# Attention scores in three fp32r products, and GLA's state-times-query product likewise in two of three token blocks

## The chip, the core and the metric

The kernel runs on one core of one Trainium2 chip. TensorE (PE) multiplies 128-row tiles into PSUM, VectorE (DVE) and ScalarE (ACT) do elementwise work and empty PSUM, GpSimd (POOL) does a little elementwise work, and SyncE (SP) issues most transfers. The metric is the device time of one execution in microseconds; lower is better.

## The reference

One layer of a decoder for 2048 new prompt tokens and 8 sequences of 8 sample tokens, width 1024, in fp32. One projection gives the inputs of two branches: grouped attention in a window of 128 with a learned sink, and gated linear attention (GLA) with a recurrent state. The branches are gated, merged, projected and normalised. The two places that matter here:

```python
# attention: 8 heads of 64 in 2 kv groups; a block of 128 queries sees 256 keys
s = jnp.einsum('bnqhgd,bnkhd->bnhgqk', qb, kband).astype(jnp.float32) * (HEAD_DIM ** -0.5)
s = s + rel_bias(rel_table, dist)
...
p = sink_softmax(s, mask, sink...)
o = jnp.einsum('bnhgqk,bnkhd->bnqhgd', p.astype(v.dtype), vband)

# GLA: 4 heads, keys of 128, values of 256, chunk by chunk
o_inter = jnp.einsum('bthk,bhkv->bthv', qt, S)
A = jnp.where(causal, jnp.einsum('bthk,bshk->bhts', qt, kt), 0.0)
o_intra = jnp.einsum('bhts,bshv->bthv', A, vc)
S = jnp.exp(b_last)[..., None] * S + jnp.einsum('bshk,bshv->bhkv', kend, vc)
```

## The kernel before

**Passes.** The big projections run as passes of products 128 by 128 by 352, several with Strassen's seven products in place of eight. Their operands are split into a high part, rounded to fp32r, and a low part, the fp32r rest (`split`: a copy on ACT, L142, and a subtraction on DVE, L143). Three fp32r products then stand for one fp32 product: high by high (L1326), high weight by low input (L1327), low weight by high input (L1328). The tokens go in three stages of 704. In stage 0 the weight operands are made and partly stored; later stages load many of them ready-made.

**Order.** PE's order is written out by hand: the groups of the passes follow each other, four steps of three products make a "tick", and other work is put between the groups by the tick in which it is due (`at`, `tick`). DVE, ACT, POOL and SP get their order from a scheduler that takes work as it falls due and hands out buffers from pools.

**Attention** runs per stage over blocks of 128 queries, seven ticks apart. For a block due at tick o: at o-7 its keys and values (`att_load`, L740, tile `kk`) and queries (`att_q`, L748, tile `zq` of tag `zs`) are loaded by SP; at o-3 `att_prep` transposes the values on PE (L763) and copies them out on DVE (L765); at o `att_scores` runs twice, for two of four query groups each. Its products are plain fp32 with 64 rows: kv group 0 on rows 0 to 63 of the array, kv group 1 on rows 64 to 127 (L777). The results are scaled and biased on DVE (L780). At o+5 `att_sil` loads the output gate (L756, tag `zs`), at o+6 `att_trans` transposes the probabilities (L809; copied out at L811 and L813), and at o+9 `att_out` multiplies by the values (L823), gates the result and stores it (L826). Block 0 sees 128 keys, the other fifteen 256. After the last block the sample tokens follow: `samp_load` takes two tiles of tag `zs`, and `samp_q` (L853) one more for the scaled query that L897 and L898 read.

**GLA** runs per stage over heads and chunks of 256 or 128 tokens, in tiles of 128. For a chunk whose first tile is due at b: `gla_load` at b-13, decays at b-8 (`gla_z`), operands at b-3 (`gla_kq`; the query times the decay is `gb`, L1060), and for each tile `gla_v` and `gla_a` when it is due, `gla_b` 5/3 of a tile's spacing later, `gla_c` 10/3 later. In `gla_b` the tile's output starts as state times query, one fp32 product of 128 rows by 256 columns (L1110, for the 60 of 64 tiles that have a state already), then six fp32r products follow (L1104): the state's increment and the part inside the chunk. DVE then makes the new state (L1118).

**Shared buffers.** Every sink of a pass takes its results from tag `fin`, ten buffers of 352 columns; so do the gates' input and the four `zg` tiles of a gate, which live for nine ticks (products at L711). PSUM has four banks for the passes (`pd`) and four for the rest (`pa`).

Of the kernel before, what the change touches and what calls it, by code (L numbers as in the profile page):

```python
# [12 lines left out]
F32 = mybir.dt.float32  # L13
# [8 lines left out]
P = 128  # L22
# [3 lines left out]
TS = 8  # L26
# [3 lines left out]
G = 4  # L30
# [27 lines left out]
def kernel(ctx, tc, io):  # L58
# [37 lines left out]
    def mt(tag, n, bufs, dt=F32, name=None):  # L96
        return M["p"].tile([P, n], dt, tag=tag, name=name or tag, bufs=bufs)
# [26 lines left out]
    def at(t, fn):  # L124
        side.setdefault(max(int(t), now[0]), []).append(fn)
# [15 lines left out]
    def split(dst_h, dst_l, src, eng=nc.vector):  # L141
        pin["a"] = nc.scalar.copy(dst_h, src)  # L142
        i = eng.tensor_tensor(dst_l, src, dst_h.bitcast(F32), ALU.subtract)  # L143
        if eng is nc.vector:
            pin["d"] = i
# [588 lines left out]
    def att_load(b):  # L734
        t0 = b * W
        k0 = 0 if b else W
        A = AS[b] = {"k0": k0}
        need(z_kv, range(2), max(t0 - W, 0), t0 + W)
        kk = A["kk"] = mt("kk", 4 * W, 2).rearrange("p (a t) -> p a t", a=2)
        nc.sync.dma_start(kk[:, :, k0:], z_kv[:, :, t0 - W + k0:t0 + W])  # L740

    def att_q(b):
        t0 = b * W
        for z in z_q:
            need(z, range(2), t0, t0 + W)
        q = AS[b]["zq"] = mt("zs", G * W, 4, name="zq").rearrange("p (g t) -> p g t", g=G)
        for j in range(2):
            nc.sync.dma_start(q[:, 2 * j:2 * j + 2], z_q[j][:, :, t0:t0 + W])  # L748

    def att_sil(b):  # L750
        t0 = b * W
        for z in z_ga:
            need(z, range(2), t0, t0 + W)
        q = AS[b]["sil"] = mt("zs", G * W, 4, name="sil").rearrange("p (g t) -> p g t", g=G)
        for j in range(2):
            nc.sync.dma_start(q[:, 2 * j:2 * j + 2], z_ga[j][:, :, t0:t0 + W])  # L756

    def att_prep(b):
        A = AS[b]
        k0 = A["k0"]  # L760
        tp = pa()
        for i in range(k0 // W, 2):
            nc.tensor.transpose(tp[:, i * P:(i + 1) * P], A["kk"][:, 1, i * P:(i + 1) * P], ident)  # L763
        vt = A["vt"] = mt("vt", 2 * P, 2).rearrange("p (b c) -> p b c", c=P)
        nc.vector.tensor_copy(vt[:, k0 // W:].rearrange("p b c -> p (b c)"), tp[:, k0:2 * P])  # L765

    def att_scores(b, g0):
        A = AS[b]
        k0 = A["k0"]
        if g0 == 0:  # L770
            for kv in range(2):
                A["s", kv] = w4(name="s").rearrange("p (g k) -> p g k", g=G)
        ps = [pa().rearrange("p (a k) -> p a k", a=2) for _ in range(2)]
        for j in range(2):
            for kv in range(2):
                r = slice(kv * HD, (kv + 1) * HD)
                mm(ps[kv][:, j, k0:], A["zq"][r, g0 + j, :], A["kk"][r, 0, k0:], start=True, stop=True,  # L777
                   tile_position=(kv * HD, 0))
        for kv in range(2):
            nc.vector.scalar_tensor_tensor(A["s", kv][:, g0:g0 + 2, k0:], ps[kv][:, :, k0:], HD ** -0.5,  # L780
                                           st1["bias", kv][:, g0:g0 + 2, k0:], ALU.mult, ALU.add)
        if g0 == 0:
            return
        nm, sm, es, rd = (small([P, NH], n) for n in ("nm", "sm", "es", "rd"))
        for kv in range(2):
            nc.vector.tensor_reduce(nm[:, kv * G:(kv + 1) * G], A["s", kv][:, :, k0:], AX.X, ALU.max, negate=True)
        nc.vector.tensor_tensor(nm, nm, nsink, ALU.min)
        for h in range(NH):
            sl = A["s", h // G][:, h % G, k0:]
            nc.scalar.activation(sl, sl, AF.Exp, bias=nm[:, h:h + 1], accum_out=sm[:, h:h + 1])  # L790
# [40 lines left out]
    def samp_load():  # L831
        for z in [z_kv] + z_q + z_ga:
            need(z, range(2), NP, NT)
        SA["kv"] = mtile("fin", name="skv")[:, :2 * NS].rearrange("p (a t) -> p a t", a=2)
        SA["kw"] = mtile("fin", name="kw")[:, :W]
        nc.sync.dma_start(SA["kv"], z_kv[:, :, NP:])
        nc.sync.dma_start(SA["kw"], z_kv[:, 0, NP - W:NP])
        SA["zq"], SA["sil"] = (mt("zs", G * W, 4, name=n)[:, :G * NS].rearrange("p (g t) -> p g t", g=G) for n in ("szq", "ssl"))
        for j in range(2):
            nc.sync.dma_start(SA["zq"][:, 2 * j:2 * j + 2], z_q[j][:, :, NP:])  # L840
            nc.sync.dma_start(SA["sil"][:, 2 * j:2 * j + 2], z_ga[j][:, :, NP:])
        kc = w4(name="kc").rearrange("p (b c) -> p b c", b=NB)
        vc = w4(name="vc").rearrange("p (b c) -> p b c", b=NB)
        nc.sync.dma_start(kc, io["ck"].rearrange("b w c -> w b c"))
        nc.sync.dma_start(vc, io["cv"].rearrange("b w c -> w b c"))
        SA["kc"], SA["vc"] = kc, vc
        nc.sync.dma_start(io["o_ks"][:, 0:W - TS, :], io["ck"][:, TS:W, :])
        nc.sync.dma_start(io["o_vs"][:, 0:W - TS, :], io["cv"][:, TS:W, :])

    def samp_q():  # L850
        qs = SA["qs"] = mt("zs", G * W, 4, name="qs")[:, :G * NS].rearrange("p (b g t) -> p b g t", g=G, t=TS)
        for g in range(G):
            nc.scalar.mul(qs[:, :, g, :], SA["zq"][:, g].rearrange("p (b t) -> p b t", t=TS), HD ** -0.5)  # L853

# [223 lines left out]
    def gla_a(B, i):  # L1078
        ts = slice(i * P, (i + 1) * P)
        ap = pa()  # L1080
        mm(ap[:, :P], B["k"][:, ts], B["q"][:, ts], start=True, stop=True)  # L1081
        A_ = rot("a")
        nc.vector.copy_predicated(A_, cmask.bitcast(U32), ap[:, :P])
        x = rot("ah")
        split(x[:, :P], x[:, P:], A_, nc.gpsimd)
        B["a", i] = x[:, :P], x[:, P:]

    def gla_norm(B, key, o, n):
# [6 lines left out]
        nc.scalar.mul(on[:n], o, sq[:n])  # L1095
        B["on", key] = on

    def gla_b(B, i):
        ts = slice(i * P, (i + 1) * P)
        gh, gl = B["gv", i]  # L1100

        def three(ps, w, x, start):
            for j, (a, c) in enumerate(((w[0], x[0]), (w[1], x[0]), (w[0], x[1]))):
                mm(ps, a, c, start=start and j == 0, stop=(j == 2))  # L1104

        gv, kT2 = (gh[:, :HV], gl[:, :HV]), (gh[:, HV:], gl[:, HV:])
        S = sstate.get(B["h"])
        op = pa()
        if S is not None:
            mm(op[:, :HV], B["qb"][:, ts], S_t[S], start=True, stop=False)  # L1110
        sp = pa()
        three(sp[:, :HV], kT2, gv, True)
        three(op[:, :HV], B["a", i], gv, S is None)
        Sn = S_free.popleft()
        if S is None:
            nc.vector.tensor_copy(S_t[Sn], sp[:, :HV])
        else:
            nc.vector.scalar_tensor_tensor(S_t[Sn], S_t[S], B["e1"][:, i:i + 1], sp[:, :HV], ALU.mult, ALU.add)  # L1118
            S_free.append(S)
        sstate[B["h"]] = Sn  # L1120
        gla_norm(B, i, op[:, :HV], P)
# [59 lines left out]
    def gla_phase(s, t0, st):  # L1181
# [5 lines left out]
        for h, (c0, T_) in ([(h, c) for c in GCH[s] for h in range(GH)] if s == 1 else  # L1187
                            [(h, c) for h in range(GH) for c in GCH[s]]):
            if True:
                last = c0 + T_ == NT  # L1190
                Tp = T_ - (NS if last else 0)
                nt = Tp // P
                B = dict(h=h, t0=c0, T=T_, Tp=Tp, nt=nt, last=last)
                tt = lambda v: b0 + st * v + 0.01
                b = tt(u)
                at(b - 13, lambda B=B: gla_load(B))
# [388 lines left out]
```

## Time and profile before

| | us |
|---|---|
| median of three runs | 1791.93 |
| lowest, highest run | 1784.84, 1792.70 |
| the profiled execution, its own time | 1783.34 |
| span of its records | 1781.6 |
| idle time of PE by the busy sum | 29.6 |

The profiled execution is one run; its span begins with the first record and ends with the last. Its TensorE clock was granted at 0.997 of full speed on the mean. A group of instructions is named by its line, engine, output and inputs; an fp32 product on PE leaves two records, an fp32r product one, and a transpose one. Matmul records overlap, so a product's cost is read from the spacing of starts or from the chain, not from a record's own length.

### The profile page before, as it was taken

To read this page: it belongs to the slowest core of one execution; us is meant where nothing else is said; L and a number is where in the kernel's file an instruction comes from. 1 tells how busy PE (TensorE), PEld (TensorE's weight loads), DVE (VectorE), ACT (ScalarE), POOL (GpSimd) and SP (SyncE) were. 2 spreads that over 40 slices of the span, in tenths; PEclk is the share of its full clock that TensorE was granted. 3 is DMA by queue.
4 is the path that set the end of the run, shared out by engine and by line. 5 is a ranking of instruction groups with operands and counts; after the bars stand their busy time and mean duration, and the time that the engine had idled before them with its cause. 6 is when DMAs were issued, how large, how long until landed. Compare 5 with 4: busy or idle time off the path is not lost.

```text
span 1781.6 us, 31643 instructions
## 1 busy us (share of the span) xinstructions
PE 1752.0 (98%) x11026; PEld 1644.8 (92%) x11026; DVE 1085.9 (61%) x2146; ACT 851.7 (48%) x2052; POOL 374.5 (21%) x522
## 2 busy tenths in 40 slices
PE   8999999998999999999999999999999999999998
PEld 8999988997999988999999998899999999998887
DVE  6656678778555466547655336635766755536666
ACT  4575656556574365446567334645533432311100
POOL 5345533454111000004211100000123132111111
PEclk9999999999999999999999999999999999999999
DMA  6789966976978987887789798779989978965531
GB/s 216 272 317 332 330 232 224 319 279 207 311 261 279 304 258 231 269 286 228 255 266 319 239 294 279 237 244 318 298 267 244 301 212 223 332 148 194 171 104 54
DMA packets 290911, 452.33 MB, mean 254 GB/s; under 512 B 29213, under 2 KB 210133, under 8 KB 290736
## 3 DMA queue, kind: packets, MB, share of 16 engines
q1 hardware_dynamic: 262896, 415.04, 70.7%
q10 hardware_dynamic: 20464, 26.24, 4.2%
q0 software_dynamic: 7392, 9.04, 3.6%
q8 instruction: 87, 1.43, 0.3%
q14 instruction: 72, 0.59, 0.1%
HBM read 297.52 MB, written 153.57 MB: 253 GB/s over the span
## 4 chain that ended last, share of the span: by engine, by line
PE 74%; DMA 2%; DVE 1%; POOL 1%; ACT 1%; issue 1%; SPq 0%; DVEq 0%; ACTq 0%; POOLq 0%
PE pd L1326 17%; PE pd L1328 17%; PE pd L1327 16%; PE pd L1389 3%; PE pd L1390 3%; PE pd L1391 3%; PE pa L1104 2%; PE pa L1110 1%; PE pa L777 1%; PE pa L823 1%; PE pa L809 1%; PE pa L1127 1%; DMA r<-ug_d 1%; PE pa L1067 1%; PE pa L1081 1%; PE pa L1326 1%
## 5 line engine op out<-in xcount | busy, mean ns | idle before, releaser
L143 DVE TENSOR_TENSOR wp<-ws,wp 128x512 fp32r<-128x512 f32 (+1 forms) x396 | 274.4, 696 | 203.9 <-ACT wp L142 192.9
L142 ACT CAST wp<-ws 128x512 fp32r<-128x512 f32 (+1 forms) x396 | 234.2, 595 | 191.8 <-PE pd L1328 127.7
L348 POOL TENSOR_TENSOR ws<-ws 128x256 f32<-128x256 f32 x162 | 144.1, 918 | 156.5 <-DVE wp L143 103.9
L143 POOL TENSOR_TENSOR ah<-aper,ah 128x128 fp32r<-128x128 f32 x64 | 37.3, 583 | 397.6 <-ACT ah L142 394.4
L384 ACT COPY m<-pd 128x352 f32<-128x352 f32 x146 | 66.1, 454 | 87.2 <-PE pd L1328 80.0
L1390 PE MATMUL pd<-woh,x 128*128 128x512 f32 (+1 forms) x272 | 102.4, 377 | 0.0
L1391 PE MATMUL pd<-wol,x 128*128 128x512 f32 (+1 forms) x272 | 102.4, 377 | 0.0
L1389 PE MATMUL pd<-woh,x 128*128 128x512 f32 (+1 forms) x272 | 102.4, 377 | 0.0
L1326 PE MATMUL pd<-x1h,wp 128*128 128x352 f32 x292 | 96.7, 331 | 2.3 <-DVE fin L405 2.2
L1326 PE MATMUL pd<-x7h,wp 128*128 128x352 f32 x292 | 97.1, 333 | 1.1 <-DVE fin L201 0.9
L1326 PE MATMUL pd<-x3h,wp 128*128 128x352 f32 x292 | 96.8, 331 | 0.3 <-DVE fin L399 0.3
L1326 PE MATMUL pd<-x5h,wp 128*128 128x352 f32 x292 | 96.6, 331 | 0.0
L1326 PE MATMUL pd<-x6h,wp 128*128 128x352 f32 x292 | 96.3, 330 | 0.0
L1326 PE MATMUL pd<-x2h,wp 128*128 128x352 f32 x292 | 96.3, 330 | 0.0
L1326 PE MATMUL pd<-x4h,wp 128*128 128x352 f32 x292 | 96.2, 330 | 0.0
L1328 PE MATMUL pd<-x1h,wp 128*128 128x352 f32 x292 | 94.0, 322 | 0.1
L1328 PE MATMUL pd<-x7h,wp 128*128 128x352 f32 x292 | 94.0, 322 | 0.0
L1328 PE MATMUL pd<-x4h,wp 128*128 128x352 f32 x292 | 93.8, 321 | 0.0
L1328 PE MATMUL pd<-x3h,wp 128*128 128x352 f32 x292 | 93.8, 321 | 0.0
L1327 PE MATMUL pd<-x7l,wp 128*128 128x352 f32 x292 | 93.8, 321 | 0.0
L1328 PE MATMUL pd<-x6h,wp 128*128 128x352 f32 x292 | 93.8, 321 | 0.0
L1328 PE MATMUL pd<-x5h,wp 128*128 128x352 f32 x292 | 93.8, 321 | 0.0
(454 smaller groups left out, 5387.9 us busy)
## 6 DMA issues: line engine op xcount, KB each, us to landing
wp<-wk_w_g SPq DMA_DIRECT2D x96, 512.0 KB
ws<-w_g SPq DMA_DIRECT2D x120, 256.0 KB
wk_w_g<-wp SPq DMA_DIRECT2D x48, 512.0 KB
wp<-wk_w_ra SPq DMA_DIRECT2D x32, 512.0 KB
wp<-wk_w_rg SPq DMA_DIRECT2D x32, 512.0 KB
ws<-w_at SPq DMA_DIRECT2D x53, 256.0 KB
wp<-wk_w_at SPq DMA_DIRECT2D x24, 512.0 KB
ws<-w_pg SPq DMA_DIRECT2D x48, 256.0 KB
```

The costliest lines, as they stand in the source:

```text
L142: pin["a"] = nc.scalar.copy(dst_h, src)
L143: i = eng.tensor_tensor(dst_l, src, dst_h.bitcast(F32), ALU.subtract)
L348: nc.gpsimd.tensor_tensor(o[:, c], x[:, c], y[:, c], op)
L384: nc.scalar.copy(A[i], ps)
L777: mm(ps[kv][:, j, k0:], A["zq"][r, g0 + j, :], A["kk"][r, 0, k0:], start=True, stop=True, tile_position=(kv * HD, 0))
L1104: mm(ps, a, c, start=start and j == 0, stop=(j == 2))
L1326: mm(ps, wh, xh[:, ts], start=first, stop=False, skip_group_check=ch)
L1327: mm(ps, wh, xl[:, ts], start=False, stop=False, skip_group_check=ch)
L1328: mm(ps, wl, xh[:, ts], start=False, stop=(k == q.kh - 1 and not (type(i) is tuple and i[1] == 0)), skip_group_check=ch)
L1389: mm(ps, xh[:, xs], hi, start=(k == 0), stop=False)
L1390: mm(ps, xl[:, xs], hi, start=False, stop=False)
L1391: mm(ps, xh[:, xs], lo, start=False, stop=(k == KT - 1))
```

## The change

Three things change.

1. `att_prep` now splits the block's queries (128 by 512) into `qh` and the rest, which overwrites `zq`, and its keys (128 by 256; 128 by 128 in block 0) into `kh` and the rest, in `kk`. `att_scores` makes three fp32r products in place of one fp32 product, in the order high-high, low query, low key, and in each of the three first kv group 0, then 1. The product of the two low parts is left out.
2. For GLA's stages 0 and 1 (`B["s"] < MS - 1`), `gla_kq` splits the decayed query into two `fin` tiles, `qbh` and `qbl`, which live until the chunk's last `gla_b`. The new `gla_s`, due a third of a tile's spacing after the preceding tile's `gla_b`, splits the head's state into `Sh` and `Sl`. In `gla_b` three fp32r products take the place of L1110. Stage 2 stays as it was.
3. Tag `zs` has three buffers instead of four.

The profile's line numbers move by up to 21 in the changed file.

```diff
     def att_q(b):
-        q = AS[b]["zq"] = mt("zs", G * W, 4, name="zq").rearrange("p (g t) -> p g t", g=G)
+        q = AS[b]["zq"] = mt("zs", G * W, 3, F32R, "zq")
+        v = q.bitcast(F32).rearrange("p (g t) -> p g t", g=G)
...
     def att_prep(b):
+        q = A["zq"]
+        x = mt("qh", G * W, 1, F32R)
+        split(x, q, q.bitcast(F32))
+        A["q"] = [t.rearrange("p (g t) -> p g t", g=G) for t in (x, q)]
+        x, y = mt("kh", 2 * W, 1, F32R), A["kk"][:, 0]
+        split(x[:, k0:], y[:, k0:], y.bitcast(F32)[:, k0:])
+        A["k"] = x, y
         vt = A["vt"] = mt("vt", 2 * P, 2).rearrange("p (b c) -> p b c", c=P)
...
     def att_scores(b, g0):
         for j in range(2):
-            for kv in range(2):
-                r = slice(kv * HD, (kv + 1) * HD)
-                mm(ps[kv][:, j, k0:], A["zq"][r, g0 + j, :], A["kk"][r, 0, k0:], start=True, stop=True,
-                   tile_position=(kv * HD, 0))
+            for n, (x, y) in enumerate(((0, 0), (1, 0), (0, 1))):
+                for kv in range(2):
+                    r = slice(kv * HD, (kv + 1) * HD)
+                    mm(ps[kv][:, j, k0:], A["q"][x][r, g0 + j, :], A["k"][y][r, k0:], start=(n == 0), stop=(n == 2),
+                       tile_position=(kv * HD, 0))
...
     def samp_q():
-        qs = SA["qs"] = mt("zs", G * W, 4, name="qs")[:, :G * NS]...
+        qs = SA["qs"] = mt("zs", G * W, 3, name="qs")[:, :G * NS]...
...
     def gla_kq(B):
+        if B["s"] < MS - 1:
+            B["qs"] = [mtile("fin", F32R, n) for n in ("qbh", "qbl")]
+            split(B["qs"][0][:, :T], B["qs"][1][:, :T], B["qb"][:, :T])
...
+    def gla_s(B):
+        S = sstate.get(B["h"])
+        if S is not None and "qs" in B:
+            B["Ss"] = [mt(n, HV, 1, F32R) for n in ("Sh", "Sl")]
+            split(*B["Ss"], S_t[S])
...
     def gla_b(B, i):
-        if S is not None:
+        if S is not None and "qs" in B:
+            three(op[:, :HV], [q[:, ts] for q in B["qs"]], B["Ss"], True, False)
+        elif S is not None:
             mm(op[:, :HV], B["qb"][:, ts], S_t[S], start=True, stop=False)
...
+                    at(tt(u + i + 1), lambda B=B: gla_s(B))
                     at(tt(u + i + 5 / 3), lambda B=B, i=i: gla_b(B, i))
```

How the instructions stand is shown at three places, before and after; a row has the line, the operation, output and inputs, and the size of the output.

PE at the scores of a block in stage 1, before (its `pa` is a PSUM tile):

```order
L1327 MATMUL pd_75<-x5l,wp 128x352
L1328 MATMUL pd_75<-x5h,wp 128x352
L777 MATMUL pa<-kk,zq 128x256 x8
L1326 MATMUL pd_76<-x5h,wp 128x352
L1327 MATMUL pd_76<-x5l,wp 128x352
```

The scores of a block with 256 keys now:

```order
L786 MATMUL pa<-kh,qh 128x256 x2
L786 MATMUL pa<-kh,zq 128x256 x2
L786 MATMUL pa<-kk,qh 128x256 x2
L786 MATMUL pa<-kh,qh 128x256 x2
L786 MATMUL pa<-kh,zq 128x256 x2
L786 MATMUL pa<-kk,qh 128x256 x2
L1347 MATMUL pd_76<-x3h,wp 128x352
```

Each row x2 is the two kv groups; here `zq` and `kk` are the low parts. Eight fp32 products have become twenty-four fp32r products, of which the last twelve are shown. They stay in one piece between the groups of the passes.

DVE in stage 0 around the copies `pT` that free PSUM ahead of the fourth block's scores, before, with the semaphores each waits for:

```order
L393 TENSOR_TENSOR fin<-m_3121,pd_77 128x352 [waits PE_49]
L395 TENSOR_TENSOR fin<-fin,u_3140 128x352 [waits DVE_49]
L401 TENSOR_TENSOR u_3140<-u_3140,pd_74 128x352 [waits DVE_49,PE_49]
L201 SCALAR_TENSOR_TENSOR fin<-th,fin 128x352 [waits Activation_49]
L402 TENSOR_TENSOR fin<-u_3140,m_3121 128x352 [waits DVE_49]
L143 TENSOR_TENSOR wp<-w_3176,wp 128x512 [waits Activation_49]
L811 COPY pT<-pa 128x512 [waits PE_49] x2
```

And now:

```order
L393 TENSOR_TENSOR fin<-m_3187,pd_77 128x352 [waits PE_49,Activation_49]
L143 TENSOR_TENSOR wp<-ws,wp 128x512 [waits DMAHW7_49,DMAHW6_49,Activation_49]
L143 TENSOR_TENSOR zq<-zq,qh 128x512 [waits DMAHW2_49,DMAHW1_49,Activation_49]
L143 TENSOR_TENSOR kk<-kk,kh 128x256 [waits DMAHW0_49,Activation_49]
L143 TENSOR_TENSOR wp<-ws,wp 128x512 [waits DMAHW3_49,Activation_49]
L395 TENSOR_TENSOR fin<-fin,u_3206 128x352 [waits DVE_49]
L820 COPY pT<-pa 128x512 [waits PE_49]
L401 TENSOR_TENSOR u_3206<-u_3206,pd_74 128x352 [waits DVE_49]
L820 COPY pT<-pa 128x512 [waits PE_49]
```

The two subtractions of the split, which wait for the loads, stand ahead of the copies; L401 has come between them, and L201, L402 and a weight split have moved behind them.

ACT at the sample tokens, where `kcT` and `vn` are copies of transposed cache keys and new values, before:

```order
L813 COPY pT<-pa 128x512 [waits PE_49] x2
L142 CAST wp<-ws 128x512
L853 ACTIVATE qs<-szq 128x8x8 x2
L853 ACTIVATE qs<-szq 128x8x8 [waits DMAHW1_49]
L853 ACTIVATE qs<-szq 128x8x8
L384 COPY m_13779<-pd_74 128x352 [waits PE_49]
```

And now:

```order
L870 COPY kcT<-pa 128x512 [waits DVE_49,PE_49]
L870 COPY kcT<-pa 128x512 [waits PE_49]
L388 COPY u_14546<-pd_77 128x352 [waits PE_49]
L142 CAST wp<-ws 128x512
L862 ACTIVATE qs<-szq 128x8x8 [waits DMAHW5_49,DMAHW4_49,DMAHW6_49,DMAHW3_49,DVE_49]
L862 ACTIVATE qs<-szq 128x8x8 x3
L891 COPY vn<-pa 8x512 [waits PE_49] x2
L388 COPY u_14600<-pd_74 128x352 [waits PE_49]
```

The scaled query has moved from ahead of the cache keys' copies to behind them, and waits for transfers, the last block's store among them.

More of the change, by code (lines that the diff above doesn't have):

```diff
@@ L738, in att_load @@
         need(z_kv, range(2), max(t0 - W, 0), t0 + W)
-        kk = A["kk"] = mt("kk", 4 * W, 2).rearrange("p (a t) -> p a t", a=2)
-        nc.sync.dma_start(kk[:, :, k0:], z_kv[:, :, t0 - W + k0:t0 + W])
+        kk = A["kk"] = mt("kk", 4 * W, 2, F32R).rearrange("p (a t) -> p a t", a=2)
+        nc.sync.dma_start(kk.bitcast(F32)[:, :, k0:], z_kv[:, :, t0 - W + k0:t0 + W])
     def att_q(b):
@@ L745, in att_q @@
             need(z, range(2), t0, t0 + W)
-        q = AS[b]["zq"] = mt("zs", G * W, 4, name="zq").rearrange("p (g t) -> p g t", g=G)
+        q = AS[b]["zq"] = mt("zs", G * W, 3, F32R, "zq")
+        v = q.bitcast(F32).rearrange("p (g t) -> p g t", g=G)
         for j in range(2):
-            nc.sync.dma_start(q[:, 2 * j:2 * j + 2], z_q[j][:, :, t0:t0 + W])
+            nc.sync.dma_start(v[:, 2 * j:2 * j + 2], z_q[j][:, :, t0:t0 + W])
     def att_sil(b):
@@ L753, in att_sil @@
             need(z, range(2), t0, t0 + W)
-        q = AS[b]["sil"] = mt("zs", G * W, 4, name="sil").rearrange("p (g t) -> p g t", g=G)
+        q = AS[b]["sil"] = mt("zs", G * W, 3, name="sil").rearrange("p (g t) -> p g t", g=G)
         for j in range(2):
@@ L762, in att_prep @@
         for i in range(k0 // W, 2):
-            nc.tensor.transpose(tp[:, i * P:(i + 1) * P], A["kk"][:, 1, i * P:(i + 1) * P], ident)
+            nc.tensor.transpose(tp[:, i * P:(i + 1) * P], A["kk"].bitcast(F32)[:, 1, i * P:(i + 1) * P], ident)
+        q = A["zq"]
[5 more added lines that the diff above has]
+        A["k"] = x, y
         vt = A["vt"] = mt("vt", 2 * P, 2).rearrange("p (b c) -> p b c", c=P)
@@ L837, in samp_load @@
         nc.sync.dma_start(SA["kw"], z_kv[:, 0, NP - W:NP])
-        SA["zq"], SA["sil"] = (mt("zs", G * W, 4, name=n)[:, :G * NS].rearrange("p (g t) -> p g t", g=G) for n in ("szq", "ssl"))
+        SA["zq"], SA["sil"] = (mt("zs", G * W, 3, name=n)[:, :G * NS].rearrange("p (g t) -> p g t", g=G) for n in ("szq", "ssl"))
         for j in range(2):
@@ L850, in samp_q @@
     def samp_q():
-        qs = SA["qs"] = mt("zs", G * W, 4, name="qs")[:, :G * NS].rearrange("p (b g t) -> p b g t", g=G, t=TS)
+        qs = SA["qs"] = mt("zs", G * W, 3, name="qs")[:, :G * NS].rearrange("p (b g t) -> p b g t", g=G, t=TS)
         for g in range(G):
@@ L1100, in gla_b, with three @@
         gh, gl = B["gv", i]
-        def three(ps, w, x, start):
+        def three(ps, w, x, start, last=True):
             for j, (a, c) in enumerate(((w[0], x[0]), (w[1], x[0]), (w[0], x[1]))):
-                mm(ps, a, c, start=start and j == 0, stop=(j == 2))
+                mm(ps, a, c, start=start and j == 0, stop=(last and j == 2))
         gv, kT2 = (gh[:, :HV], gl[:, :HV]), (gh[:, HV:], gl[:, HV:])
@@ L1192, in gla_phase @@
                 nt = Tp // P
-                B = dict(h=h, t0=c0, T=T_, Tp=Tp, nt=nt, last=last)
+                B = dict(s=s, h=h, t0=c0, T=T_, Tp=Tp, nt=nt, last=last)
                 tt = lambda v: b0 + st * v + 0.01
```

## The prediction

> **What bounds the kernel now.** I read the page's busy shares first, then the shares of the chain that ended last, then busy time by stretches, and last the chain in order of time.
>
> ```profile
> span 1781.6 us, 31643 instructions
> ...
> PE 1752.0 (98%) x11026; PEld 1644.8 (92%) x11026; DVE 1085.9 (61%) x2146; ACT 851.7 (48%) x2052; POOL 374.5 (21%) x522
> ...
> PE 74%; DMA 2%; DVE 1%; POOL 1%; ACT 1%; issue 1%; SPq 0%; DVEq 0%; ACTq 0%; POOLq 0%
> ```
>
> TensorE is busy for 98% of the span and carries 74% of the chain, so a shorter stream of products should show in the time, and work on DVE and ACT should not. By stretches that is true of most of the program only:
>
> ```profile
> 245.00:277.00 32.00, 27.98 (x164) 23.27 (x163) 24.33 (x43) 17.80 (x45) 14.51 (x16) 0.95 0.57 194
> ...
> 395.00:430.00 35.00, 28.62 (x186) 24.36 (x185) 31.43 (x57) 21.80 (x52) 19.55 (x22) 0.95 0.59 186
> 430.00:600.00 170.00, 170.00 (x1102) 165.98 (x1101) 88.16 (x197) 95.84 (x229) 25.98 (x47) 1.00 0.85 278
> 600.00:1240.00 640.00, 640.00 (x4242) 606.48 (x4241) 366.64 (x762) 347.41 (x888) 53.44 (x91) 1.00 0.83 267
> ```
>
> The columns are the length, then busy time of PE, PEld, DVE, ACT and POOL, the granted clock and DMA. From 430 to 1240 PE has no gap, with DVE and ACT a little over half busy. In two stretches of stage 0 PE goes idle for 4.0 and 6.4 us, the clock falls to 0.95, and DVE is 76% and 90% busy. There the elementwise engines set the pace.
>
> **The change, part by part.** *The scores.* In the chain's pieces, each with its length:
>
> ```profile
> 548.04 0.43 PE pa L1110 x2
> 548.47 0.72 PE pa L1104 x6
> ...
> 653.34 0.16 PE pd L1328
> 653.50 1.93 PE pa L777 x16
> 655.42 0.36 PE pd L1326
> 655.78 0.16 PE pd L1327
> ```
>
> One fp32 product with 256 moving columns (L1110, two records) takes 0.43 us, 0.215 a record. One fp32r product of the same shape (L1104) takes 0.72/6 = 0.12, so three cost 0.36, less than one fp32 product.
>
> ```profile
> L777 PEld LDWEIGHTS pa<-kk,zq x16: 182/187/187, 653.4 to 654.8; 64*128 64x128 f32 x16
> L777 PE MATMUL pa<-kk,zq x16: 376/376/480, 653.4 to 655.0; 64*128 64x256 f32 x16
> ```
>
> A block has eight score products, sixteen records. At 0.215 each they would need 3.4 us one after another; they start within 1.6. So the two kv halves, on rows 0 to 63 and 64 to 127 of the array, run side by side: 8 pairs x 0.216 = 1.73. The remaining 0.20 of the 1.93 is the entry into half-height tiles, and the 0.36 of the next L1326 against 0.16 is the exit. Both stay.
>
> After the change a block has 24 fp32r products, 12 pairs. The trace has no fp32r pair on half-height tiles. If pairs run side by side as here, a block takes 12 x 0.12 + 0.20 = 1.64, 0.29 less; if nothing does, 24 x 0.12 + 0.20 = 3.08, 1.15 more. A pair also needs two weight loads of 128 columns in 0.12 us. The fastest loads in the trace are these:
>
> ```profile
> 649.83 1.75 PE pa L809 x16
> ...
> L937 PEld LDWEIGHTS pa<-p,vn x32: 128/133/133, 1194.4 to 1195.3; 8*64 8x64 f32 x32
> L937 PE MATMUL pa<-p,vn x32: 217/218/238, 1194.4 to 1195.3; 8*64 8x32 f32 x32
> ```
>
> L937 starts 32 loads of 64 columns in 0.9 us, two at a time, so a pair each 0.058; twice the columns would be an estimated 0.116, just inside 0.12. I take the near end, since the rows show pairs side by side in this very place: 15 blocks x 0.29 = **-4.4 us**. Block 0 has 128 moving columns. Before, its 8 pairs cost 0.109 each (L809's 1.75/16, the same 128 columns), 0.87 us. No fp32r row has so few columns: 12 pairs cost from 0.9 (half of 0.12, plus a little) to 2.6 (as an fp32 product, 0.218). I take the load pace, 12 x 0.116 = 1.4: **+0.5**.
>
> *GLA's state product*, 40 tiles of 60: 0.43 becomes 0.36, **-2.9 us**, the rest of the group being fp32r already. So PE's stream is shorter by 6.8 us.
>
> *The splits.* Each is a copy on ACT and a subtraction on DVE, priced by the weight splits:
>
> ```profile
> L142 ACT CAST wp<-ws 128x512 fp32r<-128x512 f32 x348 | 215.2, 622 | 154.0 <-PE pd L1328 90.0 <-POOL ws L348 39.3 <-DMA ws<-w_pg 7.9
> L142 ACT CAST wp<-ws 128x256 fp32r<-128x256 f32 x48 | 19.1, 404 | 37.8 <-PE pd L1328 37.7
> L143 DVE TENSOR_TENSOR wp<-ws,wp 128x512 fp32r<-128x512 f32 x348 | 254.6, 734 | 189.0 <-ACT wp L142 178.0 <-DMA wp<-wk_w_g 2.4 <-DMA wk_w_at<-wp 1.9
> L143 DVE TENSOR_TENSOR wp<-ws,wp 128x256 fp32r<-128x256 f32 x48 | 19.8, 418 | 14.9 <-ACT wp L142 14.9
> ```
>
> A block adds 0.62 + 0.40 = 1.03 us on ACT and 0.73 + 0.42 = 1.15 on DVE; a state split 0.40 and 0.42, and so does a chunk's query. Over 16 blocks, 40 tiles and 24 chunks that is some 42 us on ACT and 45 on DVE. In stages 1 and 2 PE's full row covers them. The state's split is on a chain:
>
> ```profile
> 538.90 0.71 PE pa L1104 x6
> ...
> L1118 DVE SCALAR_TENSOR_TENSOR S<-S,e,pa 128x256 f32<-128x256 f32 x60 | 28.2, 470 | 23.1 <-PE pa L1104 23.0
> ```
>
> The state is ready 0.47 us after 539.6, and its next reader starts at 548.04: 8 us for 0.8 us of work. Nothing, as long as ACT's queue is not 7 us late. The query's split now makes ACT wait for its load, three ticks ahead of the scores:
>
> ```profile
> 257.17 1.42 SPq L748 DMA_DIRECT2D zq<-z_q  x2
> ...
> mg_d<-fin POOLq DMA_DIRECT2D x48, 176.0 KB, 4.8
> ```
>
> This is the latest of these loads. By the page's only row with a landing, 4.8 us, it lands by 263.4, and its scores start at 270.35. Behind ACT's wait stand the copies that free PSUM banks, so I keep it with the next term.
>
> *Stage 0.* Here the cover is missing:
>
> ```profile
> 270.35 0.70 PE L777 MATMUL pa<-kk,zq 64*128 64x256 f32 x2 [1.36 <-ACT pT L813]
> 272.61 3.44 PE L777 MATMUL pa<-kk,zq 64*128 64x256 f32 x14 [1.57 <-DVE pT L811]
> ...
> PE pa L544 <- DVE S L1118: 2.2, 1, 2.2
> ...
> PE pa L1104 <- DVE aper L1083: 2.0, 1, 2.0
> ```
>
> PE waited for the copies that free PSUM ahead of the scores; the 3.44 us for 14 records (1.7 elsewhere) are the lowered clock that followed. The first stretch gets two blocks' splits (2.3 us of DVE), the second three states and two queries (2.1). If all of it falls on the path and trips the clock twice more, at 1.7 us each, it costs 4.4 + 3.4 = 8. But the order of DVE and ACT is dealt anew, and the idle time (4.0 there) with its slow clock (1.7) may go: -6. I take **+2**.
>
> *The small buffers.* The query's halves come from "fin", ten buffers that all sinks share.
>
> ```profile
> 486.28 0.79 PE pa L711 x4
> ...
> 519.88 0.79 PE pa L711 x4
> ```
>
> At L711 the gates of the next stage are made, two per stage, inside GLA's phase. A gate holds five "fin" buffers for nine ticks (a tick is twelve products, 1.92 us). A chunk's halves are held from three ticks ahead of its first tile to 8/3 tiles later; at 9.6 us a tile (538.90 to 548.47) that is some 16 ticks, and a chunk begins every 10: two to four more. One to three are left where two sinks give eight results and four helpers in 14 ticks, each until its store has landed (4.8 us by the row above). DVE or ACT then waits for a landing with PSUM evictions behind it. Before, five were free and PE lost nothing there. A wait of 0 to 3 us at each of four gates: 0 to 12; PE's four banks absorb most, so I take **+2**.
>
> *The samples.* "zs" has three buffers instead of four, so the scaled query (L853) waits for the last block's store.
>
> ```profile
> 1162.45 0.70 ACT L853 ACTIVATE qs<-szq 128x64 f32<-128x64 f32 x4
> ...
> 1170.14 0.56 SPq L826 DMA_DIRECT2D ua_d<-sil  x1
> ...
> 1175.32 0.44 PE L897 MATMUL pa<-kcT,qs 64*32 64x128 f32 x8
> ```
>
> The store issued at 1170.14 lands at 1174.9 by 4.8 us; with 0.70 of scaling the query is ready at 1175.6, against 1175.32: **+0.3** (0 to 2).
>
> Sum: -4.4 + 0.5 - 2.9 + 2 + 2 + 0.3 = **-2.5 us**.
>
> **The rivals.** *(a) The whole gain arrives*: stage 0 and the gates cost nothing. -6.5, and with stage 0's own idle time gone -12. For it: 810 us without a gap on PE. Against: the two stretches above. *(b) Nothing lies side by side in the scores*: a load must wait until the product on its own rows is done, and the other half of the array can't hide it as it is in the same state. A pair then costs 0.116 + 0.12 = 0.236, a block 2.83 + 0.20, 1.1 more, times 15 = +16.5; with the other terms (0.5 - 2.9 + 4.3) the kernel is **18 us slower**. It decides from 1.73/12 = 0.144 us a pair on. Against it: L777's pairs follow at 0.216 with streaming alone at 0.215, so their loads were hidden; for it, only that an fp32r pair leaves half the time. The Trainium skill's page "TensorE: Matmul & The Clock Gate", under "The mechanism", says that a weight load overlaps with products in flight only where its row group differs; by that rule this rival would hold, and L777's 0.216 us speaks against it. *(c) The buffers bind*: the gates cost 10 and stage 0 costs 8; 18 - 6.5 = 12 us slower. For it, the count of one to three free buffers; against, that PE's four banks give some 4 us of slack.
>
> **How the numbers follow.** Forecast (between -6 and +6) 0.58; (a) 0.20, of which 0.14 with over 9 us; (b) 0.11; (c) 0.11. The profiled execution took 1783.34 us, the three runs 1784.84, 1791.93 and 1792.7: two lie near 1784 and two near 1792. Which of the two a median falls on is worth more than my sum, so I start from the mean of the four, 1788.2: 1788.2 - 2.5 = 1785.7. On the profile's own scale it is 1780.8. Low: 1783.3 - 7 = 1776. High: 1792.7 with some 8 of (b)'s or (c)'s cost, 1801; it leaves out about 0.15. A measurement of this kernel tells some 0.5% (9 us) from no change: faster 0.14, slower 0.22, the rest 0.64.
>
> **What would show it.** Right: score pieces of 1.6 us in the chain, one piece of nine products of 1.07 us per GLA tile instead of 0.43 + 0.72, no PE gap between 600 and 1240 outside the gates, and DVE and ACT busier by about 45 and 42 us. Wrong: score pieces of 3 us (b); waits of "fin" writers for stores near the gates, with PE idle there (c); a stretch of stage 0 that PE no longer waits in, or one with twice the idle time. A gap of a few us just ahead of L897's successor would show the samples' wait mis-sized.

## The result, and the profile after

The changed kernel is slower, by about 1%:

| | before | after |
|---|---|---|
| median, us | 1792.26 (4 runs) | 1807.19 (4 runs) |
| lowest, highest | 1784.84, 1792.70 | 1804.87, 1808.68 |
| ratio, 95% interval | | 1.0096 [1.0072, 1.0121] |
| profiled execution, span | 1783.34, 1781.6 | 1804.87, 1803.1 |

The forecast was 1785.7 with a range up to 1801. The profile of before is of one of its fastest runs, so the two profiles lie 21.5 us apart where the medians lie 15 apart; some 3 us of that stand ahead of 60 us (299 PE records there, 316 before), in code that the change does not touch; most of the kernels below show them there too.

The page of after, span, busy time and the shares of the chain:

```profile
span 1803.1 us, 32137 instructions
...
PE 1757.0 (97%) x11194; PEld 1653.8 (92%) x11194; DVE 1125.9 (62%) x2242; ACT 880.0 (49%) x2146; POOL 381.7 (21%) x522
...
PE 64%; DVE 4%; ACT 3%; DMA 3%; issue 1%; POOL 1%; SPq 0%; DVEq 0%; ACTq 0%; POOLq 0%
```

TensorE's part of the chain fell from 74% to 64%, and DVE, ACT and DMA took over 6 points of that: the kernel now waits where it did not. Busy time by stretches says where (columns as in the prediction: length, then PE, PEld, DVE, ACT, POOL, clock, DMA):

```profile
245.00:277.00 32.00, 30.21 (x218) 27.42 (x217) 25.92 (x49) 20.49 (x53) 14.52 (x18) 1.00 0.68 232
395.00:430.00 35.00, 29.39 (x192) 26.27 (x191) 30.96 (x53) 21.66 (x51) 22.81 (x24) 0.95 0.64 208
...
434.00:535.00 101.00, 96.48 (x618) 92.12 (x617) 64.04 (x145) 63.40 (x163) 19.39 (x31) 0.98 0.84 277
600.00:860.00 260.00, 260.00 (x1760) 245.99 (x1759) 172.12 (x338) 151.15 (x390) 23.98 (x32) 1.00 0.80 259
865.00:965.00 100.00, 94.25 (x573) 88.63 (x573) 55.95 (x131) 58.07 (x146) 15.57 (x28) 0.95 0.79 262
965.00:1240.00 275.00, 275.00 (x1939) 263.57 (x1938) 151.43 (x326) 147.02 (x383) 11.62 (x26) 1.00 0.84 269
```

The two stretches of stage 0 that the prediction feared are no worse (4.0 and 6.4 us idle before, 1.8 and 5.6 now). The loss is in two others, where PE of before has no gap; the same windows of before:

```profile
434.00:535.00 101.00, 101.00 (x655) 97.36 (x655) 56.48 (x132) 64.10 (x154) 18.51 (x33) 1.00 0.84 282
865.00:965.00 100.00, 100.00 (x648) 96.34 (x646) 54.10 (x127) 64.32 (x154) 13.81 (x27) 1.00 0.86 288
```

The number of records behind the x is the better measure, since it counts a slow clock too: in these 201 us PE now starts 1191 instead of 1303. At 101/655 = 0.154 us each the 112 missing ones are worth some **17 us**. ("Products" in a stretch are these records from here on. A tile's state product now leaves three records where it left two, and each of the two stretches has eight or nine of them, so a kernel with the split and a full row of PE would show some 12 records more than 655 and 648. The 17 us are rather too few than too many.) Both stretches are GLA with the gates of the next stage inside. What DVE waits for there shows the first new thing; its waits for the gate load `gin`, in the whole run, before:

```profile
DVE gb L1030 <- DMA gin<-zg_d: 9.0, 8, 4.4
```

and after (total, times, longest):

```profile
DVE gb L1039 <- DMA gin<-zg_d: 35.2, 14, 8.6
DVE fin L201 <- DMA z_ga<-fin: 2.0, 1, 2.0
```

The longest of them, in the timeline of after, first DVE, then SP:

```profile
879.67 0.41 DVE L143 TENSOR_TENSOR qbl<-gb,qbh 128x256 fp32r<-128x256 f32 x1
888.71 0.69 DVE L1039 TENSOR_TENSOR_SCAN gb<-rmask,gin 128x256 f32<-128x256 f32 x1 [8.63 <-DMA gin<-zg_d]
...
890.11 0.47 DVE L1138 SCALAR_TENSOR_TENSOR S<-S,e,pa 128x256 f32<-128x256 f32 x1
```

```profile
881.34 0.56 SPq L1018 DMA_DIRECT2D gin<-zg_d  x1
```

The scan of the next chunk (`gla_z`) stands right behind the query's split in DVE's queue and is reached at 880.1, before its load has even been issued. The load lands some 7 us later, and DVE, whose later rows wait their turn behind it, does nothing for 8.6 us. The new state behind it (L1138), whose products were done by 879.6, is made at 890.1; ACT's next decay step waits for DVE too. What PE waits for in the two stretches (total, times, longest), first 434 to 535:

```profile
PE pa L1122 <- DVE sg L1149: 2.4, 1, 2.4
PE pa L1093 <- DVE sg L1149: 1.1, 1, 1.1
PE pd L1347 <- ACT m L384: 0.9, 1, 0.9
```

and 865 to 965:

```profile
PE pd L1347 <- DMA wp<-wk_w_at: 2.0, 1, 2.0
PE pa L1093 <- ACT mg L716: 1.7, 1, 1.7
PE pa L1147 <- DVE S L1138: 1.0, 2, 0.8
PE pa L711 <- ACT mg L716: 0.7, 1, 0.7
```

Two waits of 0.2 us are left out. All but one of these are PSUM banks that DVE or ACT has not emptied. (The one, a weight load, was issued late by SP, which had waited 3.6 us for a store of `sg` to land, where it had waited 2.1 before.) The waits sum to about 10 us, and a gap can cost more than itself. Behind the weight load's:

```profile
886.17 0.64 PE L1347 MATMUL pd<-x7h,wp 128*128 128x352 f32 x1 [2.02 <-DMA wp<-wk_w_at]
...
887.19 0.50 PE L1347 MATMUL pd<-x7h,wp 128*128 128x352 f32 x1
887.48 0.50 PE L1348 MATMUL pd<-x7l,wp 128*128 128x352 f32 x1
```

Until 889.5 the products follow at 0.29 us instead of 0.16. The granted clock of these 3.3 us, the last column but two, is 0.50:

```profile
886.20:889.50 3.30, 3.30 (x11) 3.30 (x12) 0.76 (x2) 0.00 (x0) 0.00 (x0) 0.50 1.04 390
```

So 2.0 us of waiting cost about 3.5. In the kernel before, the gate load of the scan was issued at 870.75, and when DVE came to the scan, it waited for something else:

```profile
881.18 0.69 DVE L1030 TENSOR_TENSOR_SCAN gb<-rmask,gin 128x256 f32<-128x256 f32 x1 [1.80 <-PE pa L1110]
```

What held it back there was PE's fp32 product L1110, the last reader of an older `gb`: the scan writes a new `gb`, one of GLA's ten units (tag `u`), and had to wait for one. After the change the last reader of `gb` is the split's subtraction, which runs before the chunk starts, so a unit is free at once and the scheduler places the scan as early as it can. DVE's order in the two programs at the scene just shown, before (the scan is listed as SCALAR_TENSOR_TENSOR here):

```order
L1060 SCALAR_TENSOR_TENSOR gb<-zkq,gb 128x256
L1118 SCALAR_TENSOR_TENSOR S_220<-S_223,e_9868,pa 128x256
L143 TENSOR_TENSOR wp<-ws,wp 128x512
L1083 COPY_PREDICATED aper_209<-cmask,pa 128x128
L143 TENSOR_TENSOR gl<-pa,gv 128x384
L143 TENSOR_TENSOR wp<-ws,wp 128x512
L1129 TENSOR_TENSOR sg<-pa,sg 128x2x128
L1030 SCALAR_TENSOR_TENSOR gb<-rmask,gin 128x256
```

and after:

```order
L143 TENSOR_TENSOR qbl<-gb,qbh 128x256
L1039 SCALAR_TENSOR_TENSOR gb<-rmask,gin 128x256
L1044 TENSOR_TENSOR dm<-gb 128x256
L1045 TENSOR_TENSOR ek<-gb 128x256
L1138 SCALAR_TENSOR_TENSOR S_220<-S_223,e_10304,pa 128x256
L143 TENSOR_TENSOR wp<-ws,wp 128x512
L1067 TENSOR_TENSOR ek<-zkq,ek 128x256
L143 TENSOR_TENSOR Sl<-S_220,Sh 128x256
L1095 COPY_PREDICATED aper_209<-cmask,pa 128x128
L143 TENSOR_TENSOR gl<-pa,gv 128x384
L143 TENSOR_TENSOR wp<-ws,wp 128x512
L1149 TENSOR_TENSOR sg<-pa,sg 128x2x128
```

The scan (L1030, now L1039) has moved from behind the new state `S_220`, the mask, the eviction `gl`, the gating `sg` and two weight splits to ahead of all six.

Counted in PE products between a load's place in the program and its scan's, the distance was 43 to 165 in nine of stage 1's twelve chunks before, and is 13 to 27 in all but one now. So there are two suspects, both of buffers and neither of work: **A**, the halves in `fin` leave too few of these for the gates; **D**, the early free `gb` unit puts the scan ahead of its load. The rivals are **B**, the added copies and subtractions, and **C**, the attention part.

### The profile page after: what moved, and what is told of

Same layout as the page of the kernel before. It is cut to its first block, busy times and chain, and to the rows that moved or that the text cites. A ratio compares the mean times of both kernels' runs of the same rounds, so it can differ in the third digit from the quotient of the medians.

```text
span 1803.1 us, 32137 instructions
## 1 busy us (share of the span) xinstructions
PE 1757.0 (97%) x11194; PEld 1653.8 (92%) x11194; DVE 1125.9 (62%) x2242; ACT 880.0 (49%) x2146; POOL 381.7 (21%) x522
## 4 chain that ended last, share of the span: by engine, by line
PE 64%; DVE 4%; ACT 3%; DMA 3%; issue 1%; POOL 1%; SPq 0%; DVEq 0%; ACTq 0%; POOLq 0%
PE pd L1347 15%; PE pd L1349 14%; PE pd L1348 14%; PE pd L1410 3%; PE pd L1412 3%; PE pd L1411 3%; PE pa L1122 2%; PE pa L832 1%; PE pa L818 1%; PE pa L786 1%; DMA r<-ug_d 1%; DMA gin<-zg_d 1%; DVE wp L143 1%; PE pa L1147 1%; PE pa L1347 1%
## 5 line engine op out<-in xcount | busy, mean ns | idle before, releaser
L1347 PE MATMUL pd<-x7h,wp 128*128 128x352 f32 x292 | 99.3, 340 | 3.1 <-DMA wp<-wk_w_at 2.0
L1347 PE MATMUL pd<-x6h,wp 128*128 128x352 f32 x292 | 96.6, 331 | 1.9 <-ACT m L384 1.9
L1347 PE MATMUL pd<-x2h,wp 128*128 128x352 f32 x292 | 97.2, 333 | 0.2 <-DVE fin L393 0.2
L1347 PE MATMUL pd<-x5h,wp 128*128 128x352 f32 x292 | 96.7, 331 | 0.0
L1347 PE MATMUL pd<-x4h,wp 128*128 128x352 f32 x292 | 96.3, 330 | 0.0
L1349 PE MATMUL pd<-x7h,wp 128*128 128x352 f32 x292 | 95.6, 327 | 0.0
L1349 PE MATMUL pd<-x2h,wp 128*128 128x352 f32 x292 | 94.4, 323 | 0.0
L1348 PE MATMUL pd<-x2l,wp 128*128 128x352 f32 x292 | 94.4, 323 | 0.0
L1348 PE MATMUL pd<-x1l,wp 128*128 128x352 f32 x292 | 94.3, 323 | 0.0
```

The lines of the kernel that those rows point to most:

```text
L1347: mm(ps, wh, xh[:, ts], start=first, stop=False, skip_group_check=ch)
L1348: mm(ps, wh, xl[:, ts], start=False, stop=False, skip_group_check=ch)
L1349: mm(ps, wl, xh[:, ts], start=False, stop=(k == q.kh - 1 and not (type(i) is tuple and i[1] == 0)), skip_group_check=ch)
```

## The experiments

All ratios are against the kernel before, run on the same chip in the same session (medians 1788.4 to 1789.6 us there).

**The two parts alone.** First, attention without GLA's part:

```diff
     def gla_kq(B):
...
-        if B["s"] < MS - 1:
+        if B["s"] < 0:
             B["qs"] = [mtile("fin", F32R, n) for n in ("qbh", "qbl")]
```

> Only the attention part of the change: split scores and three 'zs' buffers; GLA's state product and its queries stay as before. It computes what the reference asks. Theory A (the 'fin' buffers run out while the next stage's gates are made, because the queries' halves sit in two of them for long): no halves sit in 'fin' here, so the loss is gone and only the scores' gain is left: 1784 to 1790 us (before less 3 to 6), no PE waits at the gates. Rival B (the added copies and subtractions in GLA hold up the engines' queues): the same 1784 to 1790, so this run does not tell A from B. Rival C (the attention part costs, by its splits in stage 0 or by three 'zs' buffers): 1800 to 1807.

Measured: 1785.37 us, 0.9982 [0.9963, 1.0]. Then GLA's part, with `att_prep`, `att_scores` and the four `zs` buffers of before:

> Only the GLA part of the change: split queries and states in stages 0 and 1; the scores stay fp32 and 'zs' keeps four buffers. It computes what the reference asks. A and B: all of the loss and none of the scores' gain, 1808 to 1815 us, with PE idle for 8 to 12 us at the two gate places (about 520 and 950 us). C: 1788 to 1793, since 40 products of 0.43 become 0.36.

Measured: 1807.70 us, 1.0106 [1.009, 1.0122], with 612 and 579 products in the two stretches. All of the loss is GLA's, so C falls. Attention alone is some 3 us faster, as its stream is shorter, but the interval reaches up to no change.

**Each suspect alone, in the kernel before.** A, by holding two `fin` buffers:

```diff
     def gla_kq(B):
...
+        if B["s"] < MS - 1:
+            B["hold"] = [mtile("fin", name=n) for n in ("hold0", "hold1")]
+            for t in B["hold"]:
+                nc.gpsimd.memset(t[:, :1], 0.0)
...
     def gla_norm(B, key, o, n):
...
+        if "hold" in B and key == B["nt"] - 1:
+            for t in B["hold"]:
+                nc.gpsimd.tensor_tensor(sq[:n], sq[:n], t[:n, :1], ALU.add)
```

> The kernel before, nothing of the change, but two 'fin' buffers are held per chunk from the queries' scaling to the chunk's last norm in stages 0 and 1, as the halves hold them; no copy or subtraction is added beside a one-column clear and two additions of that cleared column on POOL, which change no value. A: the loss comes by the holding alone, 1800 to 1810 us, with PE idle at the two gate places and stores awaited by DVE and ACT. B and C: 1789 to 1795, as before.

Measured: 1796.08 us, 1.003 [1.0012, 1.0049]: slower, without any split, but by a third of the loss and short of the 1800 to 1810 expected of A. (The buffers are held until the chunk's last norm, a little longer than the halves are.) D, by giving the scaled query a buffer of its own:

```diff
     def gla_kq(B):
...
-        for t, n in ((B["q"], T), (B["qb"], Tp)):
-            nc.vector.scalar_tensor_tensor(t[:, :n], zq[:, :n], HK ** -0.5, t[:, :n], ALU.mult, ALU.mult)
+        qd = mt("qd", 256, 2, F32, "qd") if B["s"] < MS - 1 else B["qb"]
+        for o, t, n in ((B["q"], B["q"], T), (qd, B["qb"], Tp)):
+            nc.vector.scalar_tensor_tensor(o[:, :n], zq[:, :n], HK ** -0.5, t[:, :n], ALU.mult, ALU.mult)
+        B["qb"] = qd
```

> The kernel before with one effect of the change alone: in stages 0 and 1 the scaled query is written into a buffer of its own (two buffers of 256 columns) instead of over 'gb', so that the 'gb' unit comes free at the scaling. No split, no held 'fin' buffer, scores and state product in fp32 as before; it computes what the reference asks. By the order the next chunk's scan then stands 14 to 17 products behind the issue of its load in most chunks, as after the change. D: 1796 to 1802 us, DVE's waits for 'gin' 25 to 36 us in all. Without D (A with B): 1786 to 1791, waits for 'gin' about 9.

Measured: 1792.49 us, 1.002 [1.0008, 1.0032]. The waits are there, more than expected, and cost less than the 1796 to 1802 expected of D:

```profile
DVE gb L1030 <- DMA gin<-zg_d: 50.7, 19, 8.9
```

Both edits together were run since the two alone explain only half of GLA's 1.06%:

> The kernel before with both effects and no split work: two 'fin' buffers held per chunk as the halves hold them, and the scaled query written into a buffer of its own, so that 'gb' comes free at the scaling. It computes what the reference asks. If the two compound by themselves: 1803 to 1809 us, as GLA's part alone. If they only add up: 1796 to 1800, and the rest of GLA's loss needs the split work behind the blocked engines.

Measured: 1800.56 us, 1.0065 [1.0045, 1.0085]; a little over the sum, within the intervals. The stretches of the three, each with the row of 434 to 535 and that of 865 to 965, show where each suspect acts. A:

```profile
434.00:535.00 101.00, 97.63 (x616) 92.92 (x616) 55.68 (x129) 61.87 (x148) 20.68 (x53) 0.98 0.84 282
865.00:965.00 100.00, 100.00 (x647) 96.36 (x646) 53.87 (x125) 62.86 (x150) 16.60 (x47) 1.00 0.84 282
```

D:

```profile
434.00:535.00 101.00, 100.51 (x650) 96.65 (x649) 57.77 (x134) 64.50 (x153) 17.60 (x31) 1.00 0.84 281
865.00:965.00 100.00, 97.73 (x618) 93.44 (x617) 50.57 (x119) 62.06 (x148) 12.48 (x27) 0.98 0.81 275
```

A with D:

```profile
434.00:535.00 101.00, 97.06 (x606) 91.92 (x605) 52.40 (x124) 58.47 (x143) 18.05 (x51) 0.98 0.84 277
865.00:965.00 100.00, 97.81 (x613) 92.89 (x612) 50.19 (x116) 60.61 (x144) 14.07 (x43) 0.98 0.80 268
```

Held `fin` buffers take 39 products in the first stretch and 1 in the second; the early scan takes 5 and 30; together 49 and 35. At 0.154 us these are 6.2, 5.4 and 12.9 us, where the ratios give 5.4, 3.6 and 11.6. (The counts are of one profiled execution each; that of A was its fastest, at 1789.36 us.) Each suspect has its place: A at the gates of stage 1, D at those of stage 2. At the first of them, in the kernel with A, a sink on DVE waits for a `fin` buffer, until a store has landed, and the gate's next products on PE (L711) start 2.3 us late behind it:

```profile
521.15 0.52 DVE L201 SCALAR_TENSOR_TENSOR fin<-th,pd 128x352 f32<-128x352 f32 x1 [3.63 <-DMA z_ga<-fin]
```

**Undoing one suspect in the changed kernel.** A in part, by splitting the queries seven ticks later, so that the halves sit in `fin` about half as long:

```diff
                 at(b - 3, lambda B=B: gla_kq(B))
+                at(b + 4, lambda B=B: gla_q(B))
```

(`gla_q` is the split, taken out of `gla_kq`; it comes four ticks after the chunk's first tile is due, and the expectation names the place wrongly.)

> The whole change, but a chunk's queries are split seven ticks later (one tick after the chunk's second tile would start, instead of three ticks ahead of its first), so that the halves sit in 'fin' for about half as long; the work is the same and computes what the reference asks. A: most of the loss goes, 1788 to 1797 us, and PE idles under 4 us at the gate places. B: the same work in the same queues, 1803 to 1809. C: 1803 to 1809.

Measured: 1797.28 us, 1.0049 [1.0032, 1.0066]. Half of the loss is gone, and the stretches have 655 and 585 products: the first is nearly whole again, the second is not, and DVE's waits for `gin` are still 33.9 us. D undone instead, by a late reader of `gb`:

```diff
     def gla_norm(B, key, o, n):
...
+        if "qs" in B and key == B["nt"] - 1:
+            nc.gpsimd.tensor_tensor(small([P, 1], "jk")[:n], sq[:n], B["qb"][:n, :1], ALU.add)
```

> The whole change, with the scaled query 'gb' kept from being freed early: in stages 0 and 1 a POOL addition in a chunk's last norm reads one column of it (into a scratch column that nothing reads), so that its unit comes free where the last fp32 product freed it in the kernel before. It computes what the reference asks. Theory D (the early free unit lets the next chunk's scan stand right behind the split in DVE's queue, ahead of the landing of its own gate load, and DVE blocks there with the states and PSUM evictions behind it): 1791 to 1798 us, DVE waits for gate loads ('gin') 9 to 14 us in all instead of 35, and only the loss of the held 'fin' buffers is left. A alone ('fin' only) or B (added work in the queues): 1803 to 1809.

> As the kernel with 'gb' kept, and the queries split seven ticks later, so that the halves sit in 'fin' for about half as long. It computes what the reference asks. D with A: both losses gone, 1784 to 1790 us, at or under the kernel before. B (the added copies and subtractions cost by themselves): 1795 to 1802.

Measured: 1804.83 us, 1.0092 [1.0054, 1.0129], and with the late split 1811.11, 1.0121 [1.0074, 1.0168]: both missed, though the waits were down to 7.7 and 6.8 us. The stream of products itself was slower everywhere, ahead of GLA too. In a stretch of stage 0 that the edit does not touch and in which PE is full, before:

```profile
150.00:200.00 50.00, 50.00 (x317) 50.00 (x316) 29.27 (x42) 25.04 (x50) 25.51 (x29) 1.00 1.00 355
```

and with `gb` kept:

```profile
150.00:200.00 50.00, 50.00 (x308) 50.00 (x308) 30.52 (x43) 23.78 (x47) 28.53 (x32) 1.00 0.98 343
```

317 products before, 308 now, at the same granted clock. The scratch column `jk` (three buffers of 32 bytes) had moved the pools behind it in memory by 96 bytes. With two buffers, 64 bytes, they lie as before modulo 64:

```diff
-            nc.gpsimd.tensor_tensor(small([P, 1], "jk")[:n], ...
+            nc.gpsimd.tensor_tensor(small([P, 1], "jk", 2)[:n], ...
```

> As the kernel with 'gb' kept, with two scratch columns instead of three, so that every other buffer lies at the same place modulo 64 bytes as in the kernel before (three scratch columns had moved the left-hand pools by 32). It computes what the reference asks. D: the waits for 'gin' are under 14 us and the loss by 'fin' is left, 1791 to 1798 us. If keeping 'gb' costs as much as it saves: 1803 to 1809, as the kernel with three columns.

> As the kernel with 'gb' kept and the queries split late, with two scratch columns instead of three. It computes what the reference asks. D with A, and the 32 bytes the cause of the miss of the kernel with three: 1784 to 1791 us. If not the 32 bytes: 1803 to 1812.

> The kernel before with one unused 32-byte buffer ahead of the left-hand pools (activations, GLA's units, attention's operands), which moves them from 32 to 0 modulo 64 bytes; weight buffers stay. One clear of 8 columns at the start is the only instruction added. It computes what the reference asks. If the place matters, as the products of the kernel with three scratch columns suggest (some 162 ns a product instead of 160, before the changed code too): 1796 to 1804 us. If not: 1786 to 1791.

Measured: 1794.28 us, 1.0037 [1.0021, 1.0054] with `gb` kept; 1794.91, 1.0024 [1.001, 1.0038] with the late split too; 1797.08, 1.0036 [1.0015, 1.0057] for the kernel before with 32 bytes ahead of the pools. The first hits: `gin` is waited for 8.5 us in all,

```profile
DVE gb L1039 <- DMA gin<-zg_d: 8.5, 7, 2.4
```

and the products are 619 and 633, the mirror image of the late split: the second stretch is mostly mended, the first is not.

```profile
434.00:535.00 101.00, 96.94 (x619) 92.55 (x618) 64.72 (x150) 63.41 (x163) 21.31 (x36) 0.98 0.84 277
865.00:965.00 100.00, 96.74 (x633) 92.52 (x631) 58.73 (x137) 64.95 (x163) 18.20 (x34) 1.00 0.84 282
```

D undone takes 0.6% off the changed kernel, three times what D alone adds to the kernel before. The second fell short of its 1784 to 1791; its stretches have 637 and 619 products, and why they aren't full was not found. The third hits: the place alone costs 0.36% (0.15 to 0.57 by its interval).

**The halves elsewhere, all split work kept.** Both halves in `u` units, none in `fin`:

```diff
-            B["qs"] = [mtile("fin", F32R, n) for n in ("qbh", "qbl")]
+            B["qs"] = [unit(F32R, n) for n in ("qbh", "qbl")]
```

> The whole change, with both halves of a query in two of GLA's ten 'u' units instead of two 'fin' buffers. It computes what the reference asks. By the order, the scan is held back by a unit again (its gate load is issued 42 to 118 products ahead in most of the chunks of stage 1, 13 to 33 ahead in four of them), and 'fin' is as free as before. D with A: 1786 to 1795 us, with DVE's waits for 'gin' between 10 and 25. B: 1800 to 1809.

and one half in each, which holds one `fin` buffer less and, by the unit it takes, holds the scan back (in stage 1 each load but the first two now stands 64 products or more ahead of its scan):

```diff
-            B["qs"] = [mtile("fin", F32R, n) for n in ("qbh", "qbl")]
+            B["qs"] = [unit(F32R, "qbh"), mtile("fin", F32R, "qbl")]
```

> The whole change, with the high half of a query in a 'u' unit, the low half in a 'fin' buffer. It computes what the reference asks. By the order each gate load is issued 64 products or more ahead of its scan, and one 'fin' buffer less is held. D with A: 1784 to 1792 us, DVE's waits for 'gin' under 14. B: 1800 to 1809.

Measured: 1792.34 us, 1.0019 [1.0001, 1.0038], with `gin` waits of 19.2 us; and **1785.93 us, 0.998 [0.9962, 0.9998]** for one half in each:

```profile
DVE gb L1039 <- DMA gin<-zg_d: 7.0, 7, 2.5
...
434.00:535.00 101.00, 98.68 (x642) 94.46 (x641) 61.04 (x145) 66.17 (x166) 18.88 (x31) 1.00 0.85 283
865.00:965.00 100.00, 97.64 (x634) 94.15 (x633) 56.42 (x134) 66.51 (x163) 14.78 (x27) 0.98 0.83 279
```

One line is changed and 1.2% come back, with every copy, subtraction and product of the change in place. So B is not the cause of the 1%. This is the version that beats both kernels, before by 0.2% only, which is no more than attention alone brings. Not all is mended: PE still idles 2.3 and 2.4 us in the two stretches, the 2.4 at one weight load (`wp<-wk_w_at`, as above). The same buffers with GLA's part alone:

> GLA's part of the change alone (scores in fp32, four 'zs' buffers), with the high half of a query in a 'u' unit and the low half in a 'fin' buffer: all its split work, gate loads issued 45 products or more ahead of the scan in stages 0 and 1, and 'fin' reused within 30 products 6 times instead of 24. It computes what the reference asks. If the split work is no cause of its own: 1785 to 1790 us. If it is: 1795 to 1802.

Measured: 1791.68 us, 1.0024 [1.0007, 1.0041], between the two ranges expected:

```profile
434.00:535.00 101.00, 98.91 (x644) 94.70 (x643) 60.52 (x145) 66.38 (x167) 18.83 (x31) 1.00 0.85 282
865.00:965.00 100.00, 99.99 (x660) 96.52 (x659) 59.75 (x141) 67.19 (x164) 14.75 (x27) 1.00 0.83 284
```

GLA's part is thus no gain even with its buffers mostly out of the way: 40 products shorter by 0.07 us should give 2.9 us, and 4 us are lost. With attention in, the same part cost nothing (0.998 against 0.9982). The second stretch is full here, with all split work in it; the first, where one half still holds a `fin` buffer, has 2.1 us of idle time. Much of the 6.7 us by which this profile is longer stands behind 1240 instead: up to 1760 PE idles 5.5 us there, where it idles 2.2 before, but 6.9 with attention alone, which is not slower. So it stays open what the split work costs by itself; the two stretches show a loss of 2 to 3 us, all of it in the first.

## Why the prediction was wrong

- *The scores: right.* A piece of the chain with all 24 products takes 1.62 us, against 1.64 forecast and 1.93 before:

```profile
625.04 1.62 PE pa L786 x24
```

  So two fp32r products lie side by side on the two halves, with their loads hidden, and rival (b), with 3.03 us a block, is out. The Trainium skill's page "TensorE: Matmul & The Clock Gate" ("The mechanism") lists a weight load as overlapping with products in flight only where its row group differs; the 1.62 us speak against it for this case. Attention alone measured -0.18%, 3.2 us of the 3.9 forecast for blocks 0 to 15, with an interval from 6.6 us faster to no change; a loss for three `zs` buffers and for stage 0's splits is not seen beside that.
- *GLA's product: right as a product.* It stands in the chain as forecast, nine products in 1.07 us:

```profile
467.58 1.07 PE pa L1122 x9
```

- *The splits: right as work.* Their rows add up to 46.9 us on DVE and 41.7 on ACT, against 45 and 42; the engines' busy time rose by 40 and 28.
- *Stage 0: within its range.* Its idle time went from 10.4 to 7.4 us in the two stretches; +2 was forecast, within -6 to +8.
- *The small buffers: the right place, the wrong size.* +2 was taken from 0 to 12, since "PE's four banks absorb most". Alone, the held buffers cost 5.4 us, at the first gates only; together with the early scan 11.6.
- *What was missing: the buffer that the change frees.* The prediction counted what the halves take and for how long, and never asked what comes free when the fp32 product no longer reads `gb`. "In stages 1 and 2 PE's full row covers" the added work was said of durations; it did not cover a queue that stands still for 8.6 us. That step failed: it had no term in the sum, and the freed unit cost 3.6 us alone, and some 10 by what came back when it was undone in the changed kernel. The state's split was put at nothing "as long as ACT's queue is not 7 us late"; in the scene above it was DVE's queue that was late, and the state came 10 us behind its products. The reader could have seen it in the order of DVE's rows, where the scan has moved ahead of six rows.
- *Rival (c)* had the right sign and one of the two mechanisms, and priced it at 12 us with a chance of 0.11. That this lies near the measured 15 is luck in part: its 8 us for stage 0 did not come, and the early scan's came in their place.

The parts sum as follows: scores -0.18%, A with D +0.65%, GLA's part with nearly neither +0.24%, together +0.7% against the measured +0.96%. The remaining 0.25% is about what the intervals leave, or the two effects cost more behind DVE and ACT queues that the splits have made longer. The 0.6% that came back with `gb` kept speaks for the latter, and so does the place: in the first stretch A with D lacks 49 products and GLA's part alone 43 (55 with the 12 above), but in the second 35 and 69 (81). How much of this is chance stays open.

## What to carry to other kernels

Where a scheduler hands out buffers, a buffer's last reader is part of the schedule: when an edit moves a read, list what is held longer *and* what comes free earlier, and look in each in-order queue for the instruction that moves forward with it and for the load that it then waits for. A wait for a free buffer can be what keeps an engine's queue in a good order. Where a loss shows as idle time of the bound engine, count its instructions per stretch against the kernel before: that gave each cause its place here, to a microsecond or two.

## What was unexpected of the hardware

TensorE's pace depended on where its operands lie in SBUF, at a granted clock of 1.00. In the 50 us from 150 on, with the same passes, PE started 317 products in the kernel before, 312 with the left-hand pools (activations) moved by 32 bytes, 308 with 96, and 315 with 64; the weight buffers stayed. The other kernels of this document, which leave the pools in place, have 314 to 317 there, so the 315 is no loss. The row with 32 bytes:

```profile
150.00:200.00 50.00, 50.00 (x312) 50.00 (x311) 31.46 (x44) 24.43 (x47) 28.64 (x32) 1.00 0.97 345
```

That is 1.6% and 2.9% a product in this stretch; from 600 to 860 us, where PE is full too, it is 0.5% (1681 products against 1690 before) and 1.3% (1734 with `gb` kept by three columns against 1756 by two). So this tuned kernel lost 0.4% by an unrelated 32-byte buffer. Whether it is the place modulo 64, the distance between activations and weights, or something else was not tried. A scratch column, put in as a probe, nearly hid that `gb` was a cause.
